# First output projection with its rows kept on chip, begun for all tiles beside the last attention group

## The chip, the cores and the metric

The kernel runs on one core of one Trainium2 chip. The metric is the device time in microseconds (us), the median of several runs. A core has a matrix engine (TensorE, PE in the profile), VectorE (DVE), ScalarE (ACT), GpSimd (POOL) and SyncE (SP, which only issues transfers). The engines run side by side, each works its own instructions in order, and semaphores tie them together.

## What is computed

Two layers of an encoder over 1024 rows of 1024 channels. Layer 0 mixes by windowed attention with 16 heads in four groups (four query heads share one key/value head), beside four heads of cross attention into a memory. The outputs of both stand side by side, 1024 + 512 channels, and one matrix brings them back to 1024. Layer 1 mixes by a gated linear recurrence. After each mixer comes a normalised sum and a channel mixer. Of the reference, what matters here:

```python
def mixer_window_attn(u, mem_kv, w_in, sink, w_out, pos):
    ...
    o = window_gqa_sink(q, k, v, sink).reshape(bsz, t, ATT_Q_W)
    return jnp.concatenate([o, memory_cross_attn(xq, mem_kv)], axis=-1) @ w_out
...
        u = rmsnorm(h, norm_g[layer, 0])
        ...
        h = h + rmsnorm(y, norm_g[layer, 1])
        f = conv_ffn(rmsnorm(h, norm_g[layer, 2]), ffn_w_in[layer], ffn_conv_w[layer],
                     ffn_conv_b[layer], ffn_w_out[layer])
```

## The kernel before

**Split products.** All large products are made with operands split in two: `split` (line 85) has ACT round a float to the matmul type (the high part) and DVE subtract it from the source (the low part); `mm3` (line 80) makes three matmuls of them, high by high, high by low, low by high. `wunit` (line 69) does the same for 1024 columns of weights: it loads them into one of four staging buffers `st`, and puts the two parts into a ring of four (`wh`, `wl`) or into a pool that is handed in (`xwh`, `xwl`).

**Order.** The program is written as a plain sequence; a scheduler orders the instructions of each engine by simulating them: what stands earlier in the program has priority, and what can't start yet lets later work pass. `tc.high_priority(AHEAD)` raises instructions by 2000 places. On the chip each engine then follows that fixed order.

**Rows.** `uh` and `ul` hold the two parts of the normalised rows, transposed: 8 blocks of 128 channels by 1024 rows. Layer 0 uses them in `proj` (line 252; queries, keys and values of a group) and in `cross_unit` (line 185; cross attention).

**`window` (line 227).** For the groups 0 to 2: `attend(g)`, then `proj(g + 1)`, with the cross attention's units inside the first three `attend`s. Then the projection's pools `psq` (PSUM: two banks `pj`, one bank `ptq`) and `ea` (SBUF: rotation tables, keys, values, the rotated queries `rq` and others) are released, and `attend(3)` follows, then `wo0.open(3, 2)`. `attend` (line 300) takes the 8 tiles of 128 rows one after the other: scores in two banks `ps`, maximum with the mask on DVE (line 318), exponentials on ACT (325), scaling (331, 333), transposes on PE (338), the product with the values into the one bank `po` (341, 342), and the sum of the two halves into `o` on ACT and DVE (344, 345). After each pair of tiles two transfers on SP's queue write 128 KB each of `o` to the DRAM tensor `oT` (line 349), which holds 12 blocks of 128 channels: two for each group of heads, then four for cross attention.

**`WOut` (line 371), the output projection of both layers.** It works in halves of 512 output columns. For each tile of 128 rows and each half, 12 blocks go through `mm3`, that is 36 matmuls of 512 columns into one PSUM bank. The blocks are taken in three groups (line 373): 0 to 5, 8 to 11 (cross attention), and 6 and 7 (attention's last group). `rows_of` (line 450) reads a group's rows from `oT`, splits them and multiplies; this is done for each tile, group and half anew.

`open(3, 2)` (line 394) begins five tiles: for tiles 3 and 4 it makes the first two groups, and ACT copies the sum into `part` (line 420); tiles 0 to 2 stay in their three banks `pb`. It stands behind `attend(3)` in the program, and so fills what attention leaves free. In lines 400 to 409 the buffers are requested in an order that decides which room of the pools before they take. `finish` (line 465) makes the rest of the first half (copies at line 485 or adds at 483 into `y0`, sums of squares), loads the second half's weights, and makes the second half tile by tile with the normalised sum (lines 506 to 511) and `norm_T` (line 107), which writes the rows for the channel mixer into `uh` and `ul`. The channel mixer's products (line 535) follow.

Of the kernel before, what the change touches and what calls it, by code (L numbers as in the profile page):

```python
# [6 lines left out]
F32 = mybir.dt.float32  # L7
# [9 lines left out]
P = 128  # L17
# [29 lines left out]
def build(tc, A, out):  # L47
# [21 lines left out]
    def wunit(src, n=1024, pl=None, eng=None):  # L69

        tg = ("wh", "wl") if pl is None else ("xwh", "xwl")
        h = (pl or ring).tile([P, 1024], F32R, tag=tg[0], name=tg[0])
        l = (pl or ring).tile([P, 1024], F32R, tag=tg[1], name=tg[1])
        raw = stg.tile([P, 1024], F32, tag="st", name="st")[:, :n]
        nc.sync.dma_start(raw, src)
        act.copy(h[:, :n], raw)  # L76
        (eng or dve).tensor_tensor(l[:, :n], raw, h[:, :n].bitcast(F32), op=ALU.subtract)  # L77
        return h, l

    def mm3(o, ah, al, bh, bl, first, last):  # L80
        pe.matmul(o, ah, bh, start=first, stop=False)  # L81
        pe.matmul(o, ah, bl, start=False, stop=False)  # L82
        pe.matmul(o, al, bh, start=False, stop=last)  # L83

    def split(h, l, src):
        act.copy(h, src)  # L86
        dve.tensor_tensor(l, src, h.bitcast(F32), op=ALU.subtract)  # L87
# [139 lines left out]
    def window():  # L227
# [72 lines left out]
        def attend(g, qkv):  # L300
            qs, kh, kl, v = qkv
            for b in range(2):
                for nn in range(4):
                    if nn % 2 == 0:
                        o = ap_.tile([64, 4, 256], F32, tag="o", bufs=2, name="o")
                    n = 4 * b + nn
                    lo, hi = max(n - 1, 0), min(n + 2, NT)
                    w = (hi - lo) * P
                    mo = (lo - (n - 1)) * P
                    sm = ap_.tile([P, 4, 384], F32, tag="sm", bufs=3, name="sm")  # L310
                    st = {x: ap_.tile([P, 4], F32, tag=x, name=x) for x in ("mx", "nm", "es", "su", "rd")}
                    for j in range(4):
                        s = psp.tile([P, 384], F32, tag="ps", bufs=2, name="ps")
                        m = slice(nn * P, (nn + 1) * P)
                        pe.matmul(s[:, :w], qs[j][b][:, m], kh[:, lo * P:hi * P], start=True, stop=False)
                        pe.matmul(s[:, :w], qs[j][b][:, m], kl[:, lo * P:hi * P], start=False, stop=True)
                        hd = 4 * g + j
                        dve.tensor_tensor_reduce(out=sm[:, j, :w], in0=s[:, :w], in1=wmask[:, mo:mo + w],
                                                 scale=1.0, scalar=sk8[:, hd:hd + 1], op0=ALU.add, op1=ALU.max,
                                                 accum_out=st["mx"][:, j:j + 1])  # L320
                    dve.tensor_scalar_mul(st["nm"], st["mx"], -0.125)
                    dve.tensor_tensor(st["es"], sk[:, 4 * g:4 * g + 4], st["nm"], op=ALU.add)
                    act.activation(st["es"], st["es"], AF.Exp)
                    for j in range(4):
                        act.activation(sm[:, j, :w], sm[:, j, :w], AF.Exp, bias=st["nm"][:, j:j + 1], scale=0.125,
                                       accum_out=st["su"][:, j:j + 1])
                    dve.tensor_tensor(st["su"], st["su"], st["es"], op=ALU.add)
                    dve.reciprocal(st["rd"], st["su"])
                    for j in range(4):
                        if j < 2:  # L330
                            act.activation(sm[:, j, :w], sm[:, j, :w], AF.Copy, scale=st["rd"][:, j:j + 1])
                        else:
                            dve.tensor_scalar_mul(sm[:, j, :w], sm[:, j, :w], st["rd"][:, j:j + 1])
                    po = psp.tile([P, 4, P], F32, tag="po", bufs=1, name="po")
                    for c in range(hi - lo):
                        tp = psp.tile([P, 4, P], F32, tag="pt", bufs=2, name="pt")
                        for j in range(4):
                            pe.transpose(tp[:, j, :], sm[:, j, c * P:(c + 1) * P], ident)
                        ph, pl = pair("p", c)
                        split(ph, pl, tp.rearrange("p a b -> p (a b)"))  # L340
                        pe.matmul(po, v[:, lo + c, :], ph, start=c == 0, stop=False)
                        pe.matmul(po, v[:, lo + c, :], pl, start=False, stop=c == hi - lo - 1)
                    ov = o[:, :, (nn % 2) * P:(nn % 2 + 1) * P]
                    act.copy(ov, po[64:])
                    dve.tensor_tensor(ov, po[:64], ov, op=ALU.add)
# [25 lines left out]
    class WOut:  # L371
# [22 lines left out]
        def open(self, npre, nsb):  # L394

            l = self.l
            self.w1 = tc.alloc_tile_pool(name=f"wa{l}", bufs=2, reuse_waits="tile")
            if self.psb is None:
                self.psb = tc.alloc_tile_pool(name=f"wopb{l}", bufs=npre, space=PSUM, reuse_waits="tile")
            self.pools = [[self.w1] for _ in range(3)]  # L400
            if l == 0:

                self.w1.tile([P, 512], F32, tag="part", bufs=nsb, name="part")
                for g in (0, 2):
                    self.operands(g)
                for _ in range(2):
                    for x in ("xwh", "xwl"):
                        self.w1.tile([P, 1024], F32R, tag=x, name=x)
                self.operands(1)
            self.load(0)  # L410
            if self.pre:
                for t in self.pre:
                    self.products(self.pre[t], t, 1, left=True)
                return
            for t in self.order[npre:npre + nsb]:
                ps = self.bank()
                self.products(ps, t, 0)
                self.products(ps, t, 1, True)
                self.part[t] = self.w1.tile([P, 512], F32, tag="part", bufs=nsb, name="part")
                act.copy(self.part[t], ps)  # L420
# [103 lines left out]

    def mmk(o, n, st, mv, first):
# [845 lines left out]
```

## Time and profile before

| What | us |
|---|---|
| Median of three runs | 2702.19 |
| Runs | 2701.62, 2702.19, 2704.5 |
| The profiled execution | 2705.6 |
| Its span, first to last instruction | 2703.8 |
| Mean granted clock of TensorE, of full | 0.992 |
| First read of `oT` by the projection | 411.4 |
| Last read of `oT` in layer 0 | 578.2 |
| Last write of `o` by attention (start of its DVE sum) | 496.6 |

Times in rows of the trace are counted from the span's start. A row of the order of time has the start, the duration, the engine (SPq, ACTq and POOLq are transfers being issued), the line of the kernel, the operation, what it writes and reads by the program's names, the shape and the count; in brackets stands the idle time of the engine before it with what ended it. Matmuls are pipelined, so that one of 512 columns lasts longer than the distance to the next.

### The profile page before, as it was taken

Reading aid. Unit: us, or ns where it says so; the run is one execution under the profiler, and the core shown is the slowest. Engines: PE = TensorE matmul, PEld = TensorE weight load, DVE = VectorE, ACT = ScalarE, POOL = GpSimd, SP = SyncE. Lnnn points to the kernel's source line nnn. Section 1 sums busy time; section 2 is a strip of 40 time slices with the busy share of each in tenths; the row PEclk is TensorE's granted clock in tenths of the full one; section 3 lists DMA queues with packets and bytes.
Section 4 is the critical chain, followed back from the end, with each engine's and each line's share of the span. In section 5 each row is a group of like instructions: output and inputs, shape, how many; then the busy total and the mean of one; then the engine's idle time right before and its main releaser. Section 6 shows DMA issues by size and latency. Waiting matters only on the chain. (4 is left out here: it accounts for less than half of the span.)

```text
span 2703.8 us, 39480 instructions
## 1 busy us (share of the span) xinstructions
PE 2626.8 (97%) x14496; PEld 2202.5 (81%) x14496; DVE 1835.5 (68%) x3042; ACT 1397.5 (52%) x2556; POOL 469.3 (17%) x520
## 2 busy tenths in 40 slices
PE   8899999999999999999999999999899999999998
PEld 7888897788888887887888888888688788888887
DVE  6487787678555655478797796878467756556447
ACT  6367666645444444455554554545454444444443
POOL 1221110211111100032233231221021111110013
PEclk9899999999999999999999999999999999999999
DMA  7574213557878757574246331111466787774656
GB/s 282 206 165 105 59 31 117 180 186 176 215 192 208 199 158 245 195 244 153 83 140 158 79 91 51 56 48 45 136 206 178 180 216 200 204 202 158 224 192 232
DMA packets 215315, 432.25 MB, mean 160 GB/s; under 512 B 20560, under 2 KB 77264, under 8 KB 209488
## 3 DMA queue, kind: packets, MB, share of 16 engines
q1 hardware_dynamic: 188128, 335.07, 37.9%
q0 software_dynamic: 24544, 90.19, 16.0%
q10 hardware_dynamic: 2448, 4.46, 0.4%
q8 instruction: 114, 1.87, 0.3%
q14 instruction: 81, 0.66, 0.1%
HBM read 335.79 MB, written 117.96 MB: 168 GB/s over the span
## 5 line engine op out<-in xcount | busy, mean ns | idle before, releaser
L87 DVE TENSOR_TENSOR wl<-st,wh 128x1024 fp32r<-128x1024 f32 (+1 forms) x238 | 263.1, 1112 | 324.2 <-ACT wh L86 310.4
L86 ACT CAST wh<-st 128x1024 fp32r<-128x1024 f32 (+1 forms) x238 | 222.5, 937 | 294.6 <-PE X L535 193.1
L81 PE MATMUL pj<-uh,wh 128*128 128x512 f32 x512 | 204.2, 399 | 3.5 <-DVE xl L87 2.5
L535 PE MATMUL X<-wl,wh 128*128 128x512 f32 x528 | 204.8, 390 | 0.7 <-DVE wl L87 0.7
L535 PE MATMUL X<-wh,wl 128*128 128x512 f32 x528 | 204.6, 389 | 0.0
L82 PE MATMUL pj<-ul,wh 128*128 128x512 f32 x512 | 203.2, 397 | 0.1
L83 PE MATMUL pj<-uh,wl 128*128 128x512 f32 x512 | 202.3, 395 | 0.0
L535 PE MATMUL X<-wh 128*128 128x512 f32 x528 | 198.8, 390 | 2.9 <-ACT c L908 2.6
L81 PE MATMUL pj<-wh,uh 128*128 128x384 f32 (+1 forms) x512 | 190.7, 373 | 2.2 <-DVE gs L1022 2.2
L82 PE MATMUL pj<-wl,uh 128*128 128x384 f32 (+1 forms) x512 | 187.9, 367 | 0.0
L83 PE MATMUL pj<-wh,ul 128*128 128x384 f32 (+1 forms) x512 | 187.5, 367 | 0.0
L77 DVE TENSOR_TENSOR wl<-st,wh 128x1024 fp32r<-128x1024 f32 (+1 forms) x92 | 119.6, 1309 | 28.9 <-ACT wh L76 27.8
L535 PE MATMUL V<-uh,wh 128*128 128x512 f32 x344 | 133.8, 389 | 0.0
L535 PE MATMUL V<-ul,wh 128*128 128x512 f32 x344 | 133.8, 389 | 0.0
L535 PE MATMUL V<-uh,wl 128*128 128x512 f32 x344 | 133.8, 389 | 0.0
L76 ACT CAST wh<-st 128x1024 fp32r<-128x1024 f32 (+1 forms) x99 | 99.9, 1016 | 56.6 <-PE pj L82 34.8
L535 PEld LDWEIGHTS X<-wh 128*128 128x128 f32 x528 | 99.1, 188 | 24.3 <-ACT c L908 3.0
L535 PEld LDWEIGHTS X<-wl,wh 128*128 128x128 f32 x528 | 99.1, 188 | 21.6 <-DVE wl L87 1.3
L81 PEld LDWEIGHTS pj<-uh,wh 128*128 128x128 f32 x512 | 96.9, 189 | 24.3 <-DVE xl L87 2.9
L535 PEld LDWEIGHTS X<-wh,wl 128*128 128x128 f32 x528 | 99.1, 188 | 20.6
L83 PEld LDWEIGHTS pj<-uh,wl 128*128 128x128 f32 x512 | 97.0, 189 | 19.3
L82 PEld LDWEIGHTS pj<-ul,wh 128*128 128x128 f32 x512 | 97.0, 189 | 18.6 <-DVE ul L87 0.4
(347 smaller groups left out, 7227.2 us busy)
## 6 DMA issues: line engine op xcount, KB each, us to landing
st<-hid SPq DMA_DIRECT2D x154, 256.0 KB, 3.1
st<-in_ffw_dram SPq DMA_DIRECT2D x108, 256.0 KB, 3.2
w2s<-in_ffw_dram POOLq DMA_DIRECT2D x24, 1024.0 KB, 8.0
st<-in_ffw_dram SPq DMA_DIRECT2D x46, 512.0 KB, 4.1
hid<-tt SPq DMA_DIRECT2D x88, 256.0 KB, 4.6
st<-w2s SPq DMA_DIRECT2D x88, 256.0 KB, 2.8
sx<-in_ffw_dram SPq DMA_DIRECT2D x84, 256.0 KB, 3.9
sy<-in_ffw_dram SPq DMA_DIRECT2D x42, 512.0 KB, 6.4
```

The source lines that it names most:

```text
L76: act.copy(h[:, :n], raw)
L77: (eng or dve).tensor_tensor(l[:, :n], raw, h[:, :n].bitcast(F32), op=ALU.subtract)
L81: pe.matmul(o, ah, bh, start=first, stop=False)
L82: pe.matmul(o, ah, bl, start=False, stop=False)
L83: pe.matmul(o, al, bh, start=False, stop=last)
L86: act.copy(h, src)
L87: dve.tensor_tensor(l, src, h.bitcast(F32), op=ALU.subtract)
L535: pe.matmul(o, x, y, start=new, stop=e, skip_group_check=not first)
```

## The change

A class `Out` takes the place of `WOut` for layer 0; layer 1 keeps `WOut`.

- Attention's last group no longer goes to DRAM: two transfers on POOL's queue put the rows of a pair of tiles into the blocks 6 and 7 of `ul`, ACT rounds them into `uh`, and DVE leaves the low part in `ul`.
- `begin` reads blocks 0 to 5 of each tile from `oT` into `ul`, splits them in place into `uh` and `ul`, multiplies them with the first half's weights into one of three banks `pb`, and has ACT copy the sum into `y0`, for all eight tiles. The reads and splits of tiles 0 and 1 are raised by 2000 places.
- `finish` makes the cross blocks (still read from `oT` and split) and the blocks 6 and 7 of each tile in six banks, and DVE adds them to `y0`. In the second half blocks 0 to 7 come from `uh` and `ul` without reading or splitting, then the cross blocks.
- `y0` moves from the pool of `finish` into the pool that takes `ea`'s room, the second set of row buffers goes, and the order of the buffers is that of their first request.

```diff
@@ attend
-                    if nn % 2 == 1:
+                    if nn % 2 == 1 and g == 3:
+                        ts_ = slice((n - 1) * P, (n + 1) * P)
+                        oh, ol = uh[:, 6:8, ts_], ul[:, 6:8, ts_]
+                        for hp in range(2):
+                            pool.dma_start(ul[hp * 64:(hp + 1) * 64, 6:8, ts_].bitcast(F32), o[:, hp::2, :])
+                        act.copy(oh, ol.bitcast(F32))
+                        dve.tensor_tensor(ol, ol.bitcast(F32), oh.bitcast(F32), op=ALU.subtract)
+                    elif nn % 2 == 1:
...
@@ window
         attend(3, cur)
-        wo0.open(3, 2)
+        wo0.open()
+        psb = tc.alloc_tile_pool(name="wopb", bufs=3, space=PSUM, reuse_waits="tile")
+        y0 = wo0.w1.tile([P, NT, 512], F32, bufs=1, name="y0")
+        wo0.begin(psb, "pb", 3, [y0[:, t, :] for t in range(NT)])
         psp.release()
...
+    class Out:
+        def __init__(self, l, src, key, order):
...
+            n = (6, 7)[l]
+            self.groups = (range(0, n), range(8, 12), range(n, 8))
+            self.units = ((0, 1, 2, 4, 5, 3), (0, 1, 2, 3, 4, 5))[l]
...
+        def read(self, t):
+            k = self.groups[0]
+            c = (slice(None), slice(0, len(k)), slice(t * P, (t + 1) * P))
+            raw = ul[c].bitcast(F32)
+            nc.sync.dma_start(raw, oT[self.l][0:len(k), :, c[2]].rearrange("k p t -> p k t"))
+            act.copy(uh[c], raw)
+            dve.tensor_tensor(ul[c], raw, uh[c].bitcast(F32), op=ALU.subtract)
+        def kept(self, ps, t, ks, first, last):
+            for i, k in enumerate(ks):
+                m = slice(t * P, (t + 1) * P)
+                wh, wl = self.us[self.b, k // 2]
+                c = slice((k % 2) * 512, (k % 2 + 1) * 512)
+                mm3(ps, uh[:, k, m], ul[:, k, m], wh[:, c], wl[:, c], first and i == 0, last and i == len(ks) - 1)
+        def cross(self, ps, t, first, last):
+            ks = self.groups[1]
+            oh, ol = [self.ops.tile([P, 4, P], F32R, tag=x, bufs=n + self.l, name=x) for x, n in (("oh", 2), ("ol", 3))]
+            raw = ol.bitcast(F32)
+            self.last_read = nc.sync.dma_start(raw, oT[self.l][8:12, :, t * P:(t + 1) * P].rearrange("k p t -> p k t"))
+            split(oh, ol, raw)
...
+        def begin(self, psb, tag, n, y0):
+            self.psb, self.y0 = psb, y0
+            self.banks += [(psb, tag)] * n
+            for t in self.order:
+                if t in self.order[:2 - 2 * self.l]:
+                    with tc.high_priority(AHEAD):
+                        self.read(t)
+                else:
+                    self.read(t)
+                ps = self.bank()
+                self.kept(ps, t, self.groups[0], True, True)
+                act.copy(y0[t], ps)
+            self.used = 0
+        def open(self):
+            self.w1 = tc.alloc_tile_pool(name=f"wa{self.l}", bufs=2, reuse_waits="tile")
+            self.ops = self.w1
+            self.load(0, self.w1)
...
+        def finish(self):
...
+            n = NT - 2 - len(self.banks)
+            psb2 = tc.alloc_tile_pool(name=f"wopc{l}", bufs=n, space=PSUM, reuse_waits="tile")
+            self.banks += [(psb2, "pb2")] * n
+            y0 = self.y0
...
+            for t in self.order:
+                ps = self.bank()
+                self.cross(ps, t, True, False)
+                self.kept(ps, t, self.groups[2], False, True)
...
+                dve.tensor_tensor(y0[t], ps, y0[t], op=ALU.add)
+                sumsq(wp, y0[t], s0[:, t:t + 1])
...
+            self.load(1, self.w1)
...
+            for t in self.order:
+                ts_ = slice(t * P, (t + 1) * P)
+                ps = self.bank()
+                self.kept(ps, t, range(8), True, False)
+                self.cross(ps, t, False, True)
...
-    wo0 = WOut(0, A["x"], "wout0", list(range(NT)))
+    wo0 = Out(0, A["x"], "wout0", list(range(NT)))
```

More of the change, by code (lines that the diff above doesn't have):

```diff
@@ L517, in finish, with bank, load, rows @@
             w2.release()
+            self.w1.release()
+    class Out:
+        def __init__(self, l, src, key, order):
+            self.l, self.src, self.key, self.order = l, src, key, order
+            self.us, self.wf, self.banks, self.used = {}, None, [], 0
+            n = (6, 7)[l]
+            self.groups = (range(0, n), range(8, 12), range(n, 8))
+            self.units = ((0, 1, 2, 4, 5, 3), (0, 1, 2, 3, 4, 5))[l]
+        def bank(self):
+            pl, tag = self.banks[self.used % len(self.banks)]
+            self.used += 1
+            return pl.tile([P, 512], F32, tag=tag, name="pb")
+        def load(self, b, pl=None, n=6):
+            for i, u in enumerate(self.units[:n]):
+                if (b, u) not in self.us:
+                    self.us[b, u] = wunit(A[self.key][b, u], pl=pl if i >= RING else None)
+            self.b = b
+        def read(self, t):
[17 more added lines that the diff above has]
+            split(oh, ol, raw)
+            for i, k in enumerate(ks):
+                wh, wl = self.us[self.b, k // 2]
+                c = slice((k % 2) * 512, (k % 2 + 1) * 512)
+                mm3(ps, oh[:, i, :], ol[:, i, :], wh[:, c], wl[:, c], first and i == 0, last and i == 3)
+        def begin(self, psb, tag, n, y0):
[15 more added lines that the diff above has]
+            self.load(0, self.w1)
+        def rows(self, wp, t):
+            x = wp.tile([P, D], F32, tag="x", bufs=2, name="x")
+            nc.sync.dma_start(x, self.src[t * P:(t + 1) * P, :])
+            return x
+        def finish(self):
+            l = self.l
+            self.wf = tc.alloc_tile_pool(name=f"wf{l}", bufs=1, side="right", reuse_waits="tile") if l == 0 else None
+            wp = tc.alloc_tile_pool(name=f"wo{l}", bufs=2, side="right", reuse_waits="tile")
+            psp = tc.alloc_tile_pool(name=f"wops{l}", bufs=2, space=PSUM, side="right", reuse_waits="tile")
+            n = NT - 2 - len(self.banks)
+            psb2 = tc.alloc_tile_pool(name=f"wopc{l}", bufs=n, space=PSUM, reuse_waits="tile")
+            self.banks += [(psb2, "pb2")] * n
+            y0 = self.y0
+            s0 = wp.tile([P, NT], F32, bufs=1, name="s0")
+            for t in self.order:
+                ps = self.bank()
+                self.cross(ps, t, True, False)
+                self.kept(ps, t, self.groups[2], False, True)
+                if t == self.order[5]:
+                    after = self.last_read
+                dve.tensor_tensor(y0[t], ps, y0[t], op=ALU.add)
+                sumsq(wp, y0[t], s0[:, t:t + 1])
+            with tc.issue_after(after.ins):
+                g1 = grow(wp, A["norm_g"][l, 1:2, :], "g1")
+                g2 = grow(wp, A["norm_g"][l, 2:3, :], "g2")
+                xs = {}
+                for t in self.order[:2]:
+                    xs[t] = self.rows(wp, t)
+            self.load(1, self.w1)
+            self.first = wunit(A["ffw1"][l, 0, :, :1024], pl=self.wf) if l == 0 else None
+            for t in self.order:
+                pool.tensor_tensor(y0[t], y0[t], g1[:, :512], op=ALU.mult)
+            for t in self.order:
+                ts_ = slice(t * P, (t + 1) * P)
+                ps = self.bank()
+                self.kept(ps, t, range(8), True, False)
+                self.cross(ps, t, False, True)
+                x = xs[t] if t in xs else self.rows(wp, t)
+                ss = wp.tile([P, 1], F32, tag="ss1", name="ss1")
+                sumsq(wp, ps, ss)
+                y1 = wp.tile([P, 512], F32, tag="y1", name="y1")
+                dve.tensor_tensor(y1, ps, g1[:, 512:], op=ALU.mult)
+                dve.tensor_tensor(ss, ss, s0[:, t:t + 1], op=ALU.add)
+                rs = rstd_of(wp, ss, 1, D, "p")
+                for c, y in ((slice(0, 512), y0[t]), (slice(512, 1024), y1)):
+                    dve.scalar_tensor_tensor(x[:, c], y, rs[:, 0:1], x[:, c], op0=ALU.mult, op1=ALU.add)
+                nc.sync.dma_start(h1d[l][ts_, :], x)
+                norm_T(wp, psp, x, g2, uh, ul, t)
+            psp.release()
+            psb2.release()
+            self.psb.release()
+            wp.release()
```

## The prediction

> **What bounds the kernel now.** I read the page first, then the busy time by stretch around the change, then the order of time on each engine there.
>
> ```profile
> span 2703.8 us, 39480 instructions
> PE 2626.8 (97%) x14496; PEld 2202.5 (81%) x14496; DVE 1835.5 (68%) x3042; ACT 1397.5 (52%) x2556; POOL 469.3 (17%) x520
> ```
>
> TensorE (PE) is busy for 97% of the span and no other engine for more than 68%. The change keeps the number of matmuls (12 key blocks, 3 products, 8 tiles, 2 halves), so it can only win or lose PE time that is now empty or slow. Where that is, the stretches show; the columns are busy time and instructions of PE, PEld, DVE, ACT and POOL, the granted PE clock, and the DMA share and rate:
>
> ```profile
> core 0: us, PE busy (x) PEld busy (x) DVE busy (x) ACT busy (x) POOL busy (x), PEclk, DMA share, GB/s
> 400.00:408.00 8.00, 7.63 (x48) 6.89 (x47) 7.95 (x12) 6.83 (x11) 4.12 (x4) 1.00 0.49 122
> 408.00:416.00 8.00, 4.98 (x24) 3.03 (x22) 7.53 (x23) 4.25 (x14) 1.14 (x2) 1.00 0.85 281
> 416.00:424.00 8.00, 6.26 (x21) 3.98 (x19) 6.33 (x25) 7.67 (x22) 0.00 (x0) 0.57 0.14 43
> 424.00:432.00 8.00, 7.10 (x24) 4.38 (x24) 7.42 (x16) 7.63 (x15) 0.00 (x0) 0.79 0.28 88
> 432.00:440.00 8.00, 8.00 (x42) 6.78 (x41) 4.87 (x16) 3.81 (x11) 0.00 (x0) 1.00 0.52 159
> 440.00:480.00 40.00, 40.00 (x203) 33.84 (x203) 28.36 (x75) 25.85 (x59) 0.00 (x0) 1.00 0.29 80
> 480.00:490.00 10.00, 9.14 (x49) 7.28 (x48) 6.40 (x15) 7.82 (x21) 0.00 (x0) 1.00 0.26 77
> 490.00:500.00 10.00, 6.81 (x33) 5.07 (x32) 4.98 (x9) 5.61 (x12) 0.00 (x0) 1.00 0.35 81
> 500.00:580.00 80.00, 80.00 (x371) 66.58 (x370) 55.12 (x84) 43.04 (x83) 18.52 (x19) 1.00 0.71 225
> 580.00:600.00 20.00, 19.02 (x96) 15.72 (x95) 16.53 (x27) 11.11 (x20) 2.20 (x4) 1.00 0.40 141
> ```
>
> The last group's attention runs from about 406 to 497, the rest of the projection to about 600. PE loses time at two places. The **front**, 408 to 432: empty 3.02 + 1.74 + 0.90 = 5.66 us, and slow besides, as the clock is 0.57 and 0.79: 6.26 x 0.43 + 7.10 x 0.21 = 4.18 us; together 9.84. The **tail**, 480 to 500: 0.86 + 3.19 = 4.05 us. From 500 to 580 PE is never empty, 0.98 us are lost by 600. So about 14 us (0.5%) are to be had, and splits or reads saved after 500 are worth nothing.
>
> Why the front is empty, in order of time (start, duration, instruction, and in brackets the idle time before it with what ended it; SPq are DMA issues):
>
> ```profile
> 409.69 1.22 DVE L77 TENSOR_TENSOR wl<-st,wh 128x1024 fp32r<-128x1024 f32 x1
> 411.35 6.59 SPq L453 DMA_DIRECT2D or<-oT  x2
> 413.68 0.45 PE L315 MATMUL ps<-kh,qs 128*128 128x384 f32 x1 [1.17 <-DVE mx L318]
> 427.61 0.84 ACT L86 CAST oh<-or 128x768 fp32r<-128x768 f32 x1
> 428.80 0.63 PE L81 MATMUL pb<-wh,oh 128*128 128x512 f32 x1
> 435.89 0.84 ACT L86 CAST oh<-or 128x768 fp32r<-128x768 f32 x1 [4.21 <-DMA or<-oT]
> 494.75 0.50 PE L341 MATMUL po<-ph,v 128*128 128x512 f32 x1 [2.02 <-DVE o L345]
> 495.08 0.40 PE L342 MATMUL po<-pl,v 128*128 128x512 f32 x1
> 498.50 0.50 PE L81 MATMUL pb<-xwh,oh 128*128 128x512 f32 x1 [1.17 <-ACT oh L86]
> ```
>
> The first projection matmul, the only work that can fill PE beside attention, starts at 428.80, right after the first split at 427.61; its read was issued at 411.35, but ACT (7.67 and 7.63 of 8 us from 416 on) and DVE (7.53, 6.33 and 7.42) were full of other work until then. At the tail PE waits once for attention itself and once for a split of rows that had just gone through DRAM.
>
> **The change part by part.**
>
> *Earlier start.* The reads of tiles 0 and 1 are raised in priority; they write into `ul`, whose columns of tile 0 and 1 are dead once group 3 is projected. What else holds the first products back is room:
>
> ```profile
> 410.83 0.21 DVE L280 TENSOR_TENSOR v<-pj,v 128x64 fp32r<-128x64 f32 x1
> 421.70 1.09 PE L286 MATMUL ptq<-ident,rq 128*128 128x128 f32 x4 [0.32 <-DVE qs L297]
> 425.24 0.59 ACT L86 CAST kh<-ptq 128x512 fp32r<-128x512 f32 x1
> 440.51 0.39 PE L81 MATMUL pb<-wh,oh 128*128 128x512 f32 x1
> 440.74 0.39 PE L82 MATMUL pb<-wl,oh 128*128 128x512 f32 x1
> 436.76 0.96 DVE L87 TENSOR_TENSOR ol<-or,oh 128x768 fp32r<-128x768 f32 x1 [1.55 <-ACT oh L86]
> ```
>
> The three `pb` banks take the place of the projection's two `pj` banks (free at about 411) and of `ptq` (free at about 426). The eight part sums `y0` lie behind the two extra weight units in the pool that follows `attn0`; laid out in order of request they cover `rq`, read last at 421.70 + 1.09 = 422.8, so no part sum leaves its bank before. Until then two banks can be filled: 2 x 6 x 3 = 36 matmuls, which start 440.74 - 440.51 = 0.23 us apart, 8.3 us of work for the 9.84 us front. Against it stand two splits (0.96 us each) put ahead on a DVE that is busy 7.53 of 8 us: attention comes 1.9 us later. I take **-6.4** (8.3 - 1.9). Bounds: 0, if nothing starts sooner; -9.8, if empty and slow time both go.
>
> The slow clock follows the thin stretch: 4.98 of 8 us busy, then 0.57. [...]
>
> *More to fill the tail with.* In these 92 us the projection now issues (count, busy, mean ns, idle before):
>
> ```profile
> L81 PE MATMUL pb<-wh,oh 128*128 128x512 f32 x40 | 16.1, 402 | 0.0
> L81 PE MATMUL pb<-xwh,oh 128*128 128x512 f32 x18 | 7.2, 403 | 0.5 <-ACT oh L86 0.5
> ```
>
> (40 + 18) x 3 = 174 matmuls, 40 us. After: 8 x 18 = 144 in the part sums, and behind them the cross products of tiles 0 to 2 (3 x 12 = 36, 8.3 us), which wait for nothing of group 3. That is 180, about as many, but without the DRAM trip before 498.50. Of the tail's 4.05 us, 2.02 are attention's own chain; I take **-2.5** (bounds 0 and -4.05).
>
> *Rows of group 3 kept.* Eight 128 KB writes go from SP to POOL's queue, and their read back goes. Nearest rows (what goes where, count, size, us to landing, of 400 to 600 and of the whole span; then POOL's busy time in such an issue, least, median and most):
>
> ```profile
> oT<-o SPq DMA_DIRECT2D x10, 128.0 KB, 2.5
> sy<-sx POOLq DMA_DIRECT2D x42, 256.0 KB, 4.2
> L643 POOL DMA_DIRECT2D sx<-in_ffw_dram x42: 867/868/972, 607.7 to 2429.3; - x42
> ```
>
> POOL is empty from 416 to 500, so nothing queues behind the two issues of 0.87 us. A pair of tiles is split about 2 x 0.87 + 4.2 + 0.6 + 0.7 = 7.2 us after its attention (2.5 in place of 4.2 at best). The last pair, done at about 497, is ready by 505; five tiles with 18 matmuls each (20 us) stand ahead of its 12. Price **0**; without that cover up to 7.2. [...]
>
> *Splits and copies.* Removed: of 48 reads and splits 24 remain (8 of 768 columns, 16 of 512), with 4 more of 512 for group 3.
>
> ```profile
> or<-oT SPq DMA_DIRECT2D x16, 384.0 KB, 3.8
> or<-oT SPq DMA_DIRECT2D x16, 256.0 KB, 3.5
> or<-oT SPq DMA_DIRECT2D x16, 128.0 KB, 3.2
> L420 ACT COPY part<-pb x2: 578/580/583, 442.2 to 450.4; 128x512 f32<-128x512 f32 x2
> L483 DVE TENSOR_TENSOR y<-pb,part x2: 684/688/691, 497.4 to 504.1; 128x512 f32<-128x512 f32 x2
> ```
>
> SP's traffic falls by 8 x 384 + 16 x 128 KB = 5.1 MB, in stretches where PE is full: **0**. Added beside attention: 8 - 2 = 6 copies of 0.58 us on ACT, three more 768-column splits and four for group 3, less five of 512. With the splits at 0.84 or 0.96 us for 768 columns and 0.6 or 0.7 for 512, ACT gains 4 to 6 us on the 63 that the stretches from 408 to 500 add up to, DVE 1 to 5 on 66: both still fit a phase that is 8 us shorter (84), but no longer loosely. Cost 0 while PE has filler; if the phase is held back by DVE, the front's gain shrinks, which is why I didn't take its full bound. After 500 eight adds of 0.69 us replace six copies, on a DVE that has 25 of 80 us free.
>
> *Second half's weights.* Now the blocks 6 and 7 come second to last in the first half and third in the second, so their weight unit must be replaced within the 18 matmuls (4.1 us) of blocks 0 to 5.
>
> ```profile
> 425.71 2.00 ACT L76 CAST xwh<-st 128x1024 fp32r<-128x1024 f32 x2
> 427.17 2.35 DVE L77 TENSOR_TENSOR xwl<-st,xwh 128x1024 fp32r<-128x1024 f32 x2
> ```
>
> Cast and rest cost 1.0 + 1.2 = 2.2 us; behind another instruction on each engine it can pass 4.1. I take **+0.5** (0 to +2.2).
>
> **Sum:** -6.4 - 2.5 + 0 + 0 + 0.5 = -8.4 us. The profiled execution took 2705.6 us (span and 1.8 around it), so 2697.2; it was 3.4 us above the median of the runs shown (2702.19), so the forecast in those terms is **2693.8**. The bounds alone: -9.8 - 4.05 = -13.9. A stop also costs a restart: the second matmul after the one at 494.75 starts 0.33 us later and not 0.23; 15 stops stand in the order of time from 406 to 500, so 1.5 us more, and the end is 2702.19 - 15.4 = 2686.8.
>
> **The rivals.** *No change: the filler comes no sooner.* ACT and DVE work in order and are full in the front (above); raised or not, the splits may end up behind attention's, and the bank and `rq` limits above say that six of eight part sums can't even start before 423. Then the front stays, the tail gains: -2.5 + 0.5 = -2, **2700.2**. For it: the split at 427.61 started 16 us after its read was issued. Against: the last `wh` unit has its rest by 409.69 + 1.22 and two banks are free by 411.
>
> *Slower: ACT waits in order for the POOL copies.* The split of a kept pair stands inside attention, ahead of the next block's exponentials in the program. If ACT's order has it right behind the pair, ACT stands for 2 x 0.87 + 4.2 = 5.9 us with the exponentials behind it. The 4.21 us at 435.89 show that ACT does wait so; PE then stayed full (8.00 of 8.00 in 432 to 440), as it had filler. It decides from the point where the filler is used up: begun early, it ends with the second or third pair, and two such waits are bare: 11.8 - 6.4 for the front + 0.5 = +5.9, **2708.1**. Against it: POOL's queue is empty, and 2.5 us in place of 4.2 leaves +2.5.
>
> [...]
>
> **How the numbers follow.** Forecast 0.58, no change 0.21, slower 0.21. A difference under 0.2% (5.4 us) can't be told from none. The forecast's own range, 2686.8 to 2696.8, lies on the faster side; the second rival lies within; the third just beyond, mostly on the slower side. Range: 2686 to 2707, which leaves out most of the third's 0.21. Faster 0.58, same 0.22, slower 0.20.
>
> **What would show it.** Right: the first `pb` product before 415 (now 428.80), PE clock near 1.00 in 416 to 424, PE empty for under 2 us in the tail, the first FFN product some 8 us sooner. Wrong: a clock of still 0.6 there (first rival); ACT waits of 4 us or more ended by the copies into `ul`, with PE empty behind them (second); an empty PE at the half's boundary, ended by DVE's weight rest.

## The result and the profile after

| | Before | After |
|---|---|---|
| Median, us (12 runs each, side by side) | 2703.06 | 2708.51 |
| Lowest to highest, us | 2698.31 to 2706.92 | 2704.3 to 2712.22 |
| Span of the profiled execution, us | 2703.8 | 2706.7 |
| First product of the channel mixer (start of its matmul), us | 597.12 | 600.93 |

The ratio is 1.0018 with an interval of 1.0011 to 1.0026: the change made the kernel slower, by about 5 us. 2693.8 was forecast. The channel mixer's first product comes 3.8 us later and the profiled span is 2.9 us longer: the loss lies ahead of that product, and behind it the profiled executions differ by 0.9 us only. The profiled execution of before (2705.6 us) lies 2.5 us above its median, that of after (2708.72) 0.2 above, so the two traces show less of a difference than the medians.

Busy time by stretch of the kernel after (columns as in the same view of before):

```profile
300.00:400.00 100.00, 95.06 (x537) 83.17 (x536) 77.33 (x212) 69.64 (x183) 6.96 (x10) 0.98 0.20 56
400.00:408.00 8.00, 7.09 (x46) 6.40 (x44) 7.12 (x10) 6.29 (x9) 4.25 (x4) 1.00 0.43 131
408.00:416.00 8.00, 5.94 (x24) 4.17 (x22) 7.36 (x20) 2.46 (x6) 2.37 (x2) 0.82 0.94 257
416.00:424.00 8.00, 5.42 (x18) 3.62 (x18) 6.94 (x21) 6.86 (x19) 0.00 (x0) 0.75 0.52 169
424.00:432.00 8.00, 5.45 (x22) 3.59 (x21) 6.00 (x18) 7.95 (x24) 0.00 (x0) 0.68 0.01 2
432.00:440.00 8.00, 8.00 (x36) 6.95 (x35) 6.80 (x12) 5.83 (x10) 0.00 (x0) 0.90 0.42 132
480.00:490.00 10.00, 10.00 (x51) 8.34 (x50) 8.42 (x22) 7.93 (x17) 1.17 (x2) 1.00 0.64 210
490.00:500.00 10.00, 9.68 (x51) 7.57 (x49) 7.22 (x16) 7.07 (x19) 0.00 (x0) 1.00 0.19 52
500.00:520.00 20.00, 16.74 (x67) 12.74 (x68) 10.08 (x13) 9.44 (x20) 8.37 (x8) 0.91 0.60 185
580.00:600.00 20.00, 20.00 (x98) 16.67 (x97) 14.13 (x23) 9.18 (x16) 2.20 (x4) 1.00 0.40 138
```

And the two stretches of before that the prediction did not show:

```profile
300.00:400.00 100.00, 96.56 (x555) 85.77 (x554) 74.76 (x211) 68.38 (x184) 5.81 (x10) 0.98 0.12 35
500.00:520.00 20.00, 20.00 (x90) 16.57 (x89) 8.92 (x10) 10.30 (x23) 8.86 (x6) 1.00 0.65 201
```

Lost PE time in a stretch is its length less the busy time, plus the busy time by what the clock lacks (416 to 424: 2.58 + 5.42 x 0.25 = 3.94). Summed so, here with three experiments that are told below (sums are of the unrounded values):

| Stretch, us | before | after | e2: banks | e5: POOL splits | e6: both |
|---|---|---|---|---|---|
| 300 to 408 | 5.7 | 7.8 | 7.4 | 7.8 | 7.8 |
| 408 to 440 (front) | 9.8 | 12.2 | 4.9 | 10.7 | 3.8 |
| 480 to 500 (tail) | 4.1 | 0.3 | 1.8 | 0.3 | 2.2 |
| 500 to 520 | 0 | 4.8 | 6.1 | 1.0 | 0.2 |
| 520 to 600 | 1.0 | 0 | 2.1 | 0 | 0 |
| Sum | 20.6 | 25.0 | 22.2 | 19.8 | 14.0 |
| First channel-mixer product | 597.1 | 600.9 | 599.8 | 595.6 | 589.1 |

Each column is one execution. That of e2 was the slowest of its eleven (2708.2 us, median 2703.92), so its column makes it look worse than its median. The five kernels that leave the front as the change has it (after, e3, e4, e5, e10) lose 10.7 to 12.3 us there, so a difference of 1.5 us between two columns says little.

The sum rises by 4.4 us, the channel mixer starts 3.8 us later: the losses explain the result. The tail is full, as forecast. The front has gained nothing (whether it lost is not sure: e7, as fast as before, loses 12.4 us there), a new hole has opened at 500 to 520, and 2 us are lost ahead of 408, where the prediction didn't look.

**The front.** ACT's casts of the first six tiles and PE's rows around the first part sum, in order of time:

```profile
345.88 0.84 ACT L564 CAST uh<-ul 128x768 fp32r<-128x768 f32 x1 [0.31 <-DMA ul<-oT]
...
396.68 0.84 ACT L564 CAST uh<-ul 128x768 fp32r<-128x768 f32 x1 [0.38 <-DMA ul<-oT]
427.23 0.79 PE L341 MATMUL po<-ph,v 128*128 128x512 f32 x1 [2.23 <-ACT ph L86]
428.02 1.09 PE L286 MATMUL ptq<-ident,rq 128*128 128x128 f32 x4
431.06 0.57 ACT L86 CAST kh<-ptq 128x512 fp32r<-128x512 f32 x1
431.66 0.69 DVE L87 TENSOR_TENSOR kl<-ptq,kh 128x512 fp32r<-128x512 f32 x1 [0.32 <-ACT kh L86]
433.77 0.40 PE L81 MATMUL pb<-wh,uh 128*128 128x512 f32 x1
```

Six tiles were split by 398.5, 35 us before the first part sum at 433.77. It starts 1.4 us behind the last use of `ptq` (cast and rest at 431.06 and 431.66), although the two `pj` banks had been free for 20 us.

**The new hole.** Rows of SP, ACT, POOL and PE around 510, in order of time:

```profile
502.91 0.82 SPq L104 DMA_DIRECT2D g<-in_norm_g_dram  x2
503.80 0.50 PE L341 MATMUL po<-ph,v 128*128 128x512 f32 x1 [0.95 <-DVE o L345]
505.04 0.58 ACT L344 COPY o<-po 64x512 f32<-64x512 f32 x1 [0.88 <-PE po L342]
506.95 1.18 POOL L350 DMA_DIRECT2D ul<-o  x2 [5.53 <-DVE o L345]
508.20 0.54 SPq L606 DMA_DIRECT2D x<-in_x_dram  x1
511.85 0.62 ACT L351 CAST uh<-ul 128x512 fp32r<-128x512 f32 x1 [6.22 <-DMA ul<-o]
512.50 0.69 DVE L352 TENSOR_TENSOR ul<-ul,uh 128x512 fp32r<-128x512 f32 x1 [6.16 <-ACT uh L351]
513.93 0.61 ACT L86 CAST oh<-ol 128x512 fp32r<-128x512 f32 x1
514.60 0.50 PE L81 MATMUL pb<-wh,oh 128*128 128x512 f32 x1 [1.41 <-ACT oh L86]
516.18 0.80 PE L81 MATMUL pb<-wh,uh 128*128 128x512 f32 x1 [0.84 <-DVE y L625]
516.77 0.63 PE L82 MATMUL pb<-wl,uh 128*128 128x512 f32 x1
```

ACT stands for 6.22 us, to 511.85, for the last pair's copy, which POOL issued at 506.95. The cross split that PE needs next (513.93) is queued behind it, and PE stops twice; then the clock is low (0.62 in 516 to 520) and a matmul takes 0.63 us instead of 0.39. DVE stands as long for the same pair's rest (6.16 us), with the add that ends PE's second stop (L625) queued behind it. Of the 4.8 us lost in 500 to 520, 1.0 is attention's own last stop (503.80), which comes later than in before and so falls behind 500; the other 3.8, 2.3 empty and 1.5 slow, follow the late copy. The norm weights and residual rows (four transfers of 512 KB from 502.91 on) are under way at the same time. ACT began nothing else in these 6.22 us, though the rows of the split at 513.93 had landed by 498.1 and its buffer was free from 507.5 on.

### The profile page after: what moved, and what is told of

Its sections match the earlier page's. It is cut to its first block, busy times and chain, and to the rows that moved or that the text cites. A ratio compares the mean times of both kernels' runs of the same rounds, so it can differ in the third digit from the quotient of the medians.

```text
span 2706.7 us, 39368 instructions
## 1 busy us (share of the span) xinstructions
PE 2629.1 (97%) x14496; PEld 2204.4 (81%) x14496; DVE 1832.2 (68%) x3028; ACT 1388.1 (51%) x2536; POOL 473.6 (17%) x528
## 5 line engine op out<-in xcount | busy, mean ns | idle before, releaser
L666 PEld LDWEIGHTS X<-wh 128*128 128x128 f32 x528 | 99.1, 188 | 22.2 <-ACT c L1039 1.5
L666 PEld LDWEIGHTS X<-wh,wl 128*128 128x128 f32 x528 | 99.1, 188 | 20.6
```

The costliest lines, as they stand in the source:

```text
L666: pe.matmul(o, x, y, start=new, stop=e, skip_group_check=not first)
```

## The experiments

The runs e1 to e4, e5 to e8 and e9 to e12 form three sets, each beside its own runs of the kernel before on the same chip; ratios are to those. Where two intervals overlap, the runs don't tell the two kernels apart.

### e1: nothing raised

```diff
-                if t in self.order[:2 - 2 * self.l]:
-                    with tc.high_priority(AHEAD):
-                        self.read(t)
-                else:
-                    self.read(t)
+                self.read(t)
```

> Edit: the reads and splits of tiles 0 and 1 are not raised. In the changed kernel the operands of tiles 0 to 5 were split by 397 us, yet the first product came at 433.8, right behind the last use of the bank ptq. Theory (bank): the three pb banks are handed over only when the whole pool of the group projections is done, so operands are not what is late; without the raise the first pb product stays at 430 to 436 and the time within 2 us of the changed kernel, 2706 to 2710. Rival (raise): the raised reads put ACT and DVE work and two ACT waits for a transfer (1.26 and 2.53 us) ahead of attention between 340 and 420, which starts attention late; without the raise PE loses 2 to 4 us less in 300 to 432 and the time is 2703 to 2706.

Measured: 1.0010 (1.0001 to 1.0019). The first part sum starts at 435.0, PE is busy 94.87 us of 300 to 400 and 16.25 of 500 to 520, all about as in the change. The raise neither opens the front nor costs what is lost.

### e2: the banks stay in the projection's pool

The pool of the projection is not released before the part sums; these take their banks from it by the same tags (two `pj`, one `ptq`).

```diff
-        psq.release()
         ea.release()
...
-        psb = tc.alloc_tile_pool(name="wopb", bufs=3, space=PSUM, reuse_waits="tile")
...
-        wo0.begin(psb, "pb", 3, [y0[:, t, :] for t in range(NT)])
+        wo0.begin(psq, [("pj", 2), ("pj", 2), ("ptq", 1)], [y0[:, t, :] for t in range(NT)])
...
```

> Edit: the part sums take the projection pool's own banks (its two pj banks and ptq, by their tags), and the pool is given back at the end, in place of a new pool in its room. Theory (bank): the first pb product moves from 433.8 to 409 to 416, before the last ptq transpose, the clock stays above 0.9 in 416 to 432 and the front loses 5 to 8 us less: 2700 to 2704. Rival (DVE): ACT and DVE hold attention back in the front, and filler taken early is missing later; the front loses at most 2 us less, or as much is lost again at 480 to 520: 2706 to 2710.

Measured: 0.9990 (0.9981 to 0.9999). In order of time, then by stretch:

```profile
411.47 0.50 PE L81 MATMUL pb<-wh,uh 128*128 128x512 f32 x1
434.66 1.07 ACT L594 COPY y<-pb 128x512 f32<-128x512 f32 x2
```

```profile
408.00:416.00 8.00, 7.49 (x39) 6.28 (x40) 7.49 (x16) 2.84 (x6) 3.47 (x4) 1.00 0.79 213
416.00:424.00 8.00, 6.65 (x33) 5.33 (x31) 3.75 (x10) 5.30 (x14) 0.00 (x0) 1.00 0.55 181
424.00:432.00 8.00, 7.08 (x31) 5.44 (x31) 7.69 (x24) 5.45 (x14) 0.00 (x0) 0.79 0.34 98
500.00:520.00 20.00, 15.80 (x63) 11.96 (x63) 9.88 (x13) 9.43 (x20) 7.92 (x8) 0.88 0.56 177
```

With the same three banks and the same operands the first part sum starts 22 us sooner, and the front's loss falls from 12.2 to 4.9 us. So the new pool held it back: none of its banks was used before the last user of the old pool was done. The record doesn't show where in the old room the three banks lay, so it stays open whether they come free only together or whether the first one lay in `ptq`'s place. The hole at 500 stays, and as the rival had it part of the 7.3 us is lost again: 2.8 us more than in the change at 480 to 520 and 2.1 more after 520, in this slowest of the eleven executions.

### e3: the kept rows split beside the cross products

ACT's cast and DVE's rest move in the program from `attend` into the first half, behind the pair's first cross split.

```diff
-                        act.copy(oh, ol.bitcast(F32))
-                        dve.tensor_tensor(ol, ol.bitcast(F32), oh.bitcast(F32), op=ALU.subtract)
...
                 self.cross(ps, t, True, False)
+                if t % 2 == 0:
+                    oh, ol = [x[:, 6:8, t * P:(t + 2) * P] for x in (uh, ul)]
+                    split(oh, ol, ol.bitcast(F32))
```

> Edit: the rounding and rest of group 3's kept rows stand in the program behind the cross products of the first tile of each pair, and no longer inside attention; the POOL copies stay. Theory (ACT in order): the hole at 512 to 520 (2.25 us empty and some 2.5 us slow) comes from ACT standing 6.2 us for the last POOL copy with cross splits behind it; now ACT doesn't stand there for more than 2 us, and the time falls by 3 to 5 us, to 2703 to 2706. Rival (copy): what counts is that the copy lands late, wherever its split stands: the hole stays above 3 us, 2706 to 2710.

Measured: 1.0009 (1.0000 to 1.0017). The edit did not do what it was meant to: in ACT's order the last pair's cast still stands ahead of the next cross split, and ACT waits 6.60 us for it (PE busy 16.49 of 20 us in 500 to 520). Place in the program alone doesn't move it; this run says nothing against the wait.

### e4: the copies on SP's queue

```diff
-                            pool.dma_start(ul[hp * 64:(hp + 1) * 64, 6:8, ts_].bitcast(F32), o[:, hp::2, :])
+                            nc.sync.dma_start(ul[hp * 64:(hp + 1) * 64, 6:8, ts_].bitcast(F32), o[:, hp::2, :])
```

> Edit: the two copies of group 3's rows into the low part are issued on SP's queue in place of POOL's, the split stays inside attention. Theory (ACT in order): the copy took 506.95 to 511.85 from its first issue to ACT's start; an SP issue lands 128 KB in 2.4 us, so ACT still stands 3.5 to 4.5 us and the hole shrinks by 1 to 3 us: 2704 to 2708. Rival (queue): POOL's software queue is all of it, ACT stands under 2 us, hole under 1 us: 2702 to 2705.

Measured: 1.0007 (0.9998 to 1.0016). The theory's numbers came: ACT stands 4.08 us for the last pair, and 3.3 us are lost in 500 to 520 instead of 4.8. PE is busy 16.67 us of them (16.74 in the change), at a clock of 1.00 instead of 0.91; 2.22 us of its idle time are attention's own, behind a wait of ACT for the third pair (0.81), and 1.07 follow the last copy. The copies landed in 2.5 us instead of 4.3, but the norm weights were issued behind them here (508.59), so the run doesn't tell the queue from the neighbours. The hole doesn't need POOL's queue.

### e5: the kept rows split on POOL

```diff
-                        act.copy(oh, ol.bitcast(F32))
-                        dve.tensor_tensor(ol, ol.bitcast(F32), oh.bitcast(F32), op=ALU.subtract)
+                        pool.tensor_copy(oh, ol.bitcast(F32))
+                        pool.tensor_tensor(ol, ol.bitcast(F32), oh.bitcast(F32), op=ALU.subtract)
```

> The change as it is, but the kept rows of the last group are split on POOL (cast and rest) instead of ACT and DVE, so that neither ACT nor DVE can stand for a copy. Theory (the hole at 500 to 520 us is ACT standing 6.22 us for the last pair's copy with the cross splits behind it): the wait at ACT goes, PE is busy for over 19.5 of the 20 us at a clock near 1.00 (16.74 at 0.91 in the change), the first FFN product comes some 4 us sooner (597 in place of 600.9), ratio to before about 1.000. Rival (the hole comes from the transfers of the norm weights and residual rows, 2.5 MB issued from 502 on, or from the late end of attention): PE still loses 4 us there, ratio stays at 1.0018.

Measured: 0.9999 (0.9990 to 1.0007). POOL in order of time, then the stretch:

```profile
505.86 1.19 POOL L350 DMA_DIRECT2D ul<-o  x2 [1.45 <-DVE o L345]
512.37 0.60 POOL L351 CAST uh<-ul 128x512 fp32r<-128x512 f32 x1 [5.32 <-DMA ul<-o]
```

```profile
500.00:520.00 20.00, 19.01 (x87) 15.46 (x86) 8.84 (x12) 9.12 (x21) 10.99 (x11) 1.00 0.64 199
```

The copy is no faster than in the change, but the engine that stands for it (5.32 us) is now POOL, behind which nothing that PE needs at once is queued. The loss in 500 to 520 falls from 4.8 to 1.0 us, and what is left is attention's own stop (0.95 us, here at 502.71). The channel mixer starts 5.3 us sooner. A late copy alone cost nothing here; the hole needs ACT and DVE to stand for it with PE's operands queued behind.

### e6: e5 and e2 together

> Kept rows split on POOL, and the part sums' banks taken inside the projection's PSUM pool as in e2. Theory (two separate losses, front and hole, that add up): first part-sum product near 411, hole gone, first FFN product near 595 to 596 (599.8 in e2), ratio to before 0.997. Rival (what one gives back the other takes, since attention's own chain sets the end of the phase): no better than e2, 0.999.

Measured: 0.9970 (0.9958 to 0.9982), 2696.38 us beside 2704.92. By stretch:

```profile
408.00:416.00 8.00, 8.00 (x41) 6.70 (x40) 6.30 (x17) 2.34 (x5) 2.39 (x2) 1.00 0.86 239
416.00:424.00 8.00, 6.33 (x29) 4.54 (x28) 5.37 (x14) 5.96 (x17) 0.00 (x0) 0.99 0.49 167
424.00:432.00 8.00, 7.38 (x31) 5.68 (x31) 7.79 (x24) 6.93 (x17) 0.00 (x0) 0.80 0.09 26
500.00:520.00 20.00, 19.79 (x87) 16.38 (x88) 9.12 (x12) 8.15 (x20) 10.94 (x11) 1.00 0.60 198
```

The two losses add up: from 1.0018, e2 takes 0.28%, e5 0.19%, and e6 0.48%. The channel mixer starts at 589.1, where 595 to 596 was expected, 11.8 us sooner than in the change and 8.0 sooner than in before; the ratio is the one expected. This version beats both kernels.

### e7: before, with the banks of e2

```diff
-        psq.release()
         ea.release()
         attend(3, cur)
+        wo0.psb, wo0.cyc = psq, [("pj", 2), ("pj", 2), ("ptq", 1)]
         wo0.open(3, 2)
...
```

> The kernel before with nothing of the change, but with its three banks of the output projection taken inside the projection's PSUM pool. Theory (the first product of the output projection waits for the whole projection pool, in before too, not for its operands): first product well before 428.8, at 415 to 420, since its first read is issued at 411.35; the front's loss of 9.8 us falls to 5 or less, ratio 0.998. Rival (before's front is set by its splits, which wait behind attention's on ACT and DVE): first product still after 425, ratio 1.000.

Measured: 1.0002 (0.9993 to 1.0010); the rival held. In order of time:

```profile
411.07 6.49 SPq L457 DMA_DIRECT2D or<-oT  x2
428.41 0.84 ACT L86 CAST oh<-or 128x768 fp32r<-128x768 f32 x1
429.64 0.39 PE L81 MATMUL pb<-wh,oh 128*128 128x512 f32 x1
```

In before the rows are read at 411.07 and split at 428.41 on a full ACT, so free banks are worth nothing there. The change removes that limit (the splits of its first six tiles are done by 398.5), and only then do the banks decide: early splits alone and free banks alone bring nothing.

### e8: the last group through DRAM again

The change, but with the last group written to `oT` as in before, read back once into `ul` and split behind the pair's first cross split.

```diff
...
+                if t % 2 == 0:
+                    ts_ = slice(t * P, (t + 2) * P)
+                    oh, ol = uh[:, 6:8, ts_], ul[:, 6:8, ts_]
+                    nc.sync.dma_start(ol.bitcast(F32), oT[0][6:8, :, ts_].rearrange("k p t -> p k t"))
+                    split(oh, ol, ol.bitcast(F32))
```

> The change with only its no-DRAM part undone: the last group goes through DRAM by SP's queue as before, is read back once into the normalised rows' room and split beside the cross products of the first half. Theory (the kept rows' split inside attention makes ACT stand): no ACT wait over 3 us ended by a copy, hole at 500 to 520 down from 4.8 us of lost PE time to 1 or 2, front as in the change (first product 433), ratio 1.0005. Rival (the direct copies are harmless): hole and ratio as in the change, 1.0018; if the trip through DRAM is what cost the tail in before, PE loses 2 us or more at 500 to 505 instead.

Measured: 1.0019 (1.0010 to 1.0029), as the change; the theory's numbers did not come. In order of time:

```profile
510.84 0.62 ACT L86 CAST uh<-ul 128x512 fp32r<-128x512 f32 x1 [4.74 <-DMA ul<-oT]
512.03 0.50 PE L81 MATMUL pb<-wh,oh 128*128 128x512 f32 x1 [2.16 <-ACT oh L86]
```

ACT stands here too, 4.74 us for the read from DRAM in place of 6.22 for the direct copy, and PE stops for 2.16 us behind it (3.3 us are lost in 500 to 520). The direct copy as such neither gained nor lost anything that these runs can tell; what costs is a split of the last pair's rows ahead of ready ones on ACT, whichever way the rows come.

### e9: tiles 6 and 7 split on POOL

`read` splits the last two tiles with `pool.tensor_copy` and `pool.tensor_tensor`, the others as before.

> The change, with the early rows of tiles 6 and 7 (read at 410.3 us, behind group 2's last write) split on POOL instead of ACT and DVE. Theory (a second in-order wait of the same kind makes the front longer: ACT stands 2.53 us at 416.00 for the read of tile 6, ahead of the last group's casts): the last projection transposes come at 425 to 426 in place of 428.0, first product at 431 in place of 433.8, the front loses 10 to 11 us in place of 13, ratio to before 1.0008. Rival (that wait is ACT's slack, DVE sets the front): transposes and ratio unchanged, 428 and 1.0018.

Measured: 1.0016 (1.0008 to 1.0025), first part sum at 433.87; the rival's ratio held. The last projection transposes come at 427.2, nearer to the rival's 428 than to 425 to 426, and the front loses 13.0 us. ACT's wait for the read of tile 6 isn't what makes the front long.

### e10: the norm weights and residual rows later

```diff
-                if t == self.order[5]:
+                if t == self.order[7]:
                     after = self.last_read
```

> The change, with the transfers of the norm weights and the first residual rows ordered behind the cross read of the eighth tile instead of the sixth. Theory (the hole is the in-order split; these transfers only make the last copy land later, 4.5 us against 2.3): ACT's wait falls from 6.2 to 4 to 4.5 us, the hole's loss from 4.8 to about 3, ratio to before 1.0012. Rival (contention with these 2.5 MB is the hole's cause): copy lands in 2.5 us, hole under 1 us, ratio 1.0003 or less.

Measured: 1.0003 (0.9994 to 1.0012). In order of time, then by stretch:

```profile
511.55 0.62 ACT L351 CAST uh<-ul 128x512 fp32r<-128x512 f32 x1 [4.88 <-DMA ul<-o]
```

```profile
500.00:520.00 20.00, 18.06 (x80) 13.73 (x80) 9.92 (x15) 10.32 (x22) 2.35 (x4) 1.00 0.37 92
```

The wait, 4.88 us, lies nearer to the theory's 4 to 4.5, but the ratio and the landing (2.5 us, 4.3 for the last pair in the change) are the rival's. Of the 1.9 us lost in 500 to 520, 1.3 fall ahead of 508 and are attention's own; behind the copy 0.7 are lost, against 3.8 in the change. ACT still stands in order, but 1.3 us less, and PE's operands last nearly that long: the first 36 matmuls behind attention run from 505.89 to 514.3. So the hole has two causes that need each other, a wait in order and a landing made late by the transfers beside it (2 MB, not 2.5); with one of the two taken away (e5, e10) it is nearly gone. The interval doesn't separate this ratio from the change's.

### e11: e6, with tiles 6 and 7 on POOL too

> The kernel of e6 (kept rows split on POOL, banks inside the projection's pool), with tiles 6 and 7 of the early rows split on POOL as well. Theory (ACT's wait of 4.75 us at 415.5 is on attention's path there too): 1 to 2 us sooner than e6, front's loss 5.3 to 4, ratio to before 0.9963. Rival (part sums fill PE over that wait): 0.997 as in e6.

Measured: 0.9965 (0.9953 to 0.9978). It can't be told from e6. In its one trace the clock stays at 1.00 through the front, which loses 2.2 us (3.8 in e6).

### e12: e6, with all eight tiles' early splits on POOL

> The kernel of e6 with the early rows of all eight tiles split on POOL. Theory (the splits of tiles 0 to 5 on ACT and DVE at 345 to 397 delay groups 2 and 3: PE busy 95.0 us of 300 to 400 in place of 96.5 in before): PE busy there 96 or more, the front starts 1 to 1.5 us sooner, ratio to before 0.996 or less. Rival (POOL works in order as well, and the rotation's sums for group 3, which need 3.0 us for a tile, stand behind casts that wait for reads): PE busy under 94.5 in 300 to 400, ratio 0.998 or more.

Measured: 0.9980 (0.9970 to 0.9990). By stretch, then in order of time:

```profile
300.00:400.00 100.00, 96.37 (x549) 84.84 (x548) 78.91 (x211) 68.13 (x184) 21.84 (x22) 0.98 0.20 57
424.00:432.00 8.00, 2.37 (x11) 1.39 (x12) 6.99 (x24) 7.93 (x24) 0.00 (x0) 0.79 0.00 0
```

```profile
417.44 0.39 PE L83 MATMUL pb<-wh,ul 128*128 128x512 f32 x1
431.42 2.05 PE L338 MATMUL pt<-ident,sm 128*128 128x128 f32 x8 [5.29 <-ACT sm L331]
433.26 1.06 PE L286 MATMUL ptq<-ident,rq 128*128 128x128 f32 x4
436.74 1.07 ACT L598 COPY y<-pb 128x512 f32<-128x512 f32 x2
```

The theory's first number held: with the splits off ACT and DVE, PE is busy 96.37 us of 300 to 400, nearly the 96.56 of before, against 95.06 in the change. But the gain is gone again by 432. The three banks' 54 products were used up at 417.44, no part sum left its bank before the last read of `rq` (433.26), and with no filler left PE stood still for 5.29 us behind attention's own chain on ACT. The ratio came out where the rival had it, by another mechanism than the rival's.

## Why the prediction was wrong

**Front, -6.4: the step that failed is "Until then two banks can be filled".** It took each bank as handed over when its own last reader was done, and listed this as the argument against the first rival ("two banks are free by 411"). The change's front lost 12.16 us in place of 9.84: +2.3 in these two traces, where -6.4 was forecast. e2 shows the new pool to be the limit: with the old pool's banks taken singly the first part sum starts at 411.47 and the front's loss is 4.9 us. e6 loses 3.8, that is -6.0 against before: the size was about right for a kernel in which the banks come free one by one. That the new pool waits for `ptq` is what e2 and the place of the first part sum show together; how the allocator records it stays open. The delay of attention inside this term, 1.9 us, was too small as well: the last transposes of `rq` start at 428.02 in place of 421.70. Neither e1 (429.2) nor e9 (427.2) brings them back; 2 us were already lost ahead of 408, the rest stays open.

**The first rival** ("the filler comes no sooner") named the right outcome at the front. Its reason, splits behind attention's on ACT, holds in before (e7) and not in the change, whose first six splits were early.

**Why no part sum leaves its bank before `rq` is read**: the runs agree with this limit. The first copy into `y0` starts at 434.66 in e2 and 436.74 in e12, behind the last transposes each time; in e12 the three banks were full and PE stood for 5.29 us. No run moves this limit alone.

**Tail, -2.5:** 0.3 us are lost in 480 to 500 in place of 4.1. Attention ended later, so that its last stop, 1.0 us, fell behind 500; with it the term measures -2.7. Sign, reason and size held.

**Rows kept, price 0: the second step that failed is "five tiles with 18 matmuls each (20 us) stand ahead of its 12".** It counted the cover in PE's work and not in what PE needs from ACT and DVE. Each of those tiles needs a cross split. Two had theirs when ACT's wait began, the others stood behind the waiting cast: PE had 36 matmuls, 8.3 us (504.84 to 513.2), not 20, then stopped. Price measured: 3.8 us (4.8 less attention's own 1.0), within the 7.2 given "without that cover". The landing itself was sized rightly (4.2 assumed, 4.3 for the last pair). The second rival had the mechanism and the size of one wait (5.9; 6.22 measured), but placed it at two pairs inside attention; it came once, at the last pair. That its 2708.1 lies so near the measured 2708.51 is luck: it held two bare waits and a front won by 6.4 us, and neither came. e5 shows the mechanism by moving the wait alone, e10 by shortening the landing alone.

**Splits beside attention, cost 0:** sized on 408 to 500, while six of the eight splits ran at 345 to 397, beside groups 2 and 3's projection. PE is busy 1.5 us less there, and e12, with these splits on POOL, gives back 1.3 of them.

**POOL's queue:** issues took less than assumed (the first pair's two 1.26 us together, 0.87 each assumed). The copies landed later than from SP's queue (median of the eight 2.9 us, 2.4 in e4), which no run lays to one cause.

**Second half's weights, +0.5:** nothing was lost; PE is full at 580 to 600, 1.0 us better than before, which the sum hadn't counted as a gain.

**The sum** as measured in lost PE time: +2.3 (front) - 2.7 (tail) + 3.8 (last pair) + 2.0 (300 to 408) - 1.0 (580 to 600) = +4.4, where -8.4 was forecast. e6, with both failed steps mended, comes to 0.9970, or -8 us with an interval of -11 to -5. That this meets the forecast is in part luck: in lost PE time e6 wins 6.6 us, as -6.0 (front), -1.9 (tail), +0.2 (last pair), +2.0 (300 to 408) and -1.0 (580 to 600), and the sum had neither of the last two.

## What to carry to other kernels

Where a new pool takes an old one's room, ask which old buffer its first piece waits for, at worst the last of the whole pool; taking the buffers from the old pool by its own tags was worth 0.28% here, and nothing in the kernel whose operands came late. Count the cover of a late transfer on each engine that stands in order, and only what has its operands already: a split that waits for it holds back the ready splits behind it (ACT stood for 6.22 us here), whatever work the matrix engine still seems to have. An idle engine with a queue of its own, here POOL (5.32 us in e5, with 1.0 us lost in 500 to 520 in place of 4.8), is a good place for such a wait, as long as nothing urgent follows there.

## What was not expected of the hardware

- The clock was 0.82, 0.75 and 0.68 in the three stretches from 408 to 432, where PE was busy 5.94, 5.42 and 5.45 of 8 us and its longest single stop was 2.23 us (at 427.23); in 440 to 480, where PE was full, it was 1.00.
- The same two copies of 128 KB let ACT stand 6.22 us with four 512 KB loads issued around them and 4.88 us without (landing in 4.3 and 2.5 us).
- POOL does a cast of 128x512 in 0.60 us, as ACT does (0.62), so moving the split's first half there cost no time of its own (one of e5's four casts took 1.52 us); the rest takes POOL 1.28 to 1.63 us there, DVE 0.68 in the change.
